# Rotary embedding on one core: the last load in two halves, and GpSimd's first store held until the first half has landed

## The chip, the cores and the metric

The kernel runs on one core of a Trainium2 chip. The metric is the device time of one execution in microseconds (us), as the median of a few executions. The profile shows the core's engines: VectorE (DVE), ScalarE (ACT), GpSimd (POOL), SyncE (SP), and 16 DMA engines that copy between HBM and the on-chip memory SBUF.

## The reference

```python
def reference(x, freqs, positions):          # x: (8, 8, 1024, 64) float32
    half = x.shape[-1] // 2
    angles = np.outer(positions, freqs)
    cos, sin = np.cos(angles), np.sin(angles)
    x_first, x_second = x[..., :half], x[..., half:]
    out_first = x_first * cos - x_second * sin
    out_second = x_first * sin + x_second * cos
    return np.concatenate([out_first, out_second], axis=-1).astype(np.float32)
```

It reads 16.8 MB and writes 16.8 MB, with a handful of operations per element.

## The kernel before

The input is cut into 8 tiles of 128 partitions, each partition with C = 64 rows of 64 numbers. GpSimd loads each tile with one DMA that turns float32 into bf16 on the way. VectorE makes four operations per tile, and GpSimd stores the bf16 result with one DMA that turns it back into float32. All these DMAs go through one queue, q0. Two small pieces travel as float32 over SyncE's hardware queue: the first 16 rows of tile 0 and the last 16 rows of tile 7.

```python
    for g in range(ntiles):                                   # 8 loads, queued at once
        lo = 0 if g else head
        nc.gpsimd.dma_start(out=xts[g][:, lo:], in_=hbm(x, g, lo))
    ...                                                       # sin and cos tables
    for g in [1, 0] + list(range(2, ntiles)):
        hi = C if g < ntiles - 1 else C - tail
        ot = opool.tile([P, C, d], bf16, name="ot")[:, :hi]
        rotate(g, 0, hi, ot)                                  # four VectorE operations
        ots.append(ot)
        nc.gpsimd.dma_start(out=hbm(out, g, 0, hi), in_=ot)   # 8 stores, in the same queue
    ...
    for r in range(0, tail, piece):                           # the last 16 rows, by SyncE
        ...
            sp.dma_start(out=hbm(out, ntiles - 1, lo, lo + piece), in_=last[:, r:r + piece])
```

## Time and profile before

| | |
|---|---|
| time, median | 85.18 us (85.12 to 85.28, 3 runs) |
| span of the profiled execution | 83.4 us |
| share of the 16 DMA engines' time taken by q0 | 95.0% |
| VectorE busy | 61.9 us (74%) |
| loads, stores as seen by the engines | 218 GB/s of bf16, 430 GB/s of float32 |

How to read it: the busiest compute engine is idle for a quarter of the span, and the DMA engines are idle only at its two ends.

The trace records every packet that a DMA engine moved, with start and length. A software DMA over 128 partitions gives each of the 16 engines 8 data packets and one packet of 4 bytes that raises the semaphore. Sorted by time, the 4-byte packets of q0 fall into groups of 16, one group for each DMA. The last of a group belongs to the **slowest engine**, and the distance from group to group is what the DMA cost on it. The records carry no engine number: the slowest engine is the last of 16, and a "mean gap" is the mean start of the first 16 store packets less the mean end of the 16 semaphore packets before them.

### The profile page before, as it was taken

How to read it: one execution, taken by the hardware profiler on the slowest of the kernel's cores; microseconds unless marked ns; L12 is line 12 of the kernel's file. 1: busy time of each engine (PE TensorE's matmuls, PEld its weight loads, DVE VectorE, ACT ScalarE, POOL GpSimd, SP SyncE). 2: the span in 40 equal slices, each digit the busy share in tenths (PEclk: the TensorE clock that was granted, in tenths of full speed). 3: DMA queues.
4: the chain of work that ended last, by engine and by line, in shares of the span. 5: the costliest groups of instructions: out<-in, count | busy, mean ns of one | idle time of the engine just before them, and what ended most of it. 6: DMA issues, size and time to landing. Idle time of an engine off the chain costs nothing.

```text
span 83.4 us, 149 instructions
## 1 busy us (share of the span) xinstructions
DVE 61.9 (74%) x48; ACT 9.3 (11%) x6; POOL 8.7 (10%) x20
## 2 busy tenths in 40 slices
DVE  1023996079999999999999999999999999500000
ACT  0000049999000000000000000000000000000000
POOL 4960000000000210000200200200200202000000
DMA  0799999999999999999999999999999999999991
GB/s 0 180 205 250 237 209 220 220 193 228 208 232 208 220 220 193 228 208 232 200 385 432 393 464 401 472 409 448 432 393 464 401 479 401 448 432 417 413 384 44
DMA packets 2920, 25.44 MB, mean 305 GB/s; under 512 B 344, under 2 KB 360, under 8 KB 1000
## 3 DMA queue, kind: packets, MB, share of 16 engines
q0 software_dynamic: 2304, 24.38, 95.0%
q1 hardware_dynamic: 576, 1.05, 3.8%
q10 hardware_dynamic: 40, 0.01, 0.1%
HBM read 16.79 MB, written 16.78 MB: 403 GB/s over the span
## 4 chain that ended last, share of the span: by engine, by line
DVE 53%; issue 13%; DMA 12%; ACT 7%; SPq 1%; DVEq 1%; ACTq 0%
DVE ot L113 20%; DMA x<-in_x_dram 12%; DVE t L112 11%; DVE ot L115 11%; DVE ot L114 8%; ACT sin_h L97 2%; ACT L97 2%; ACT L102 2%; DVE last L113 1%; ACT xt L102 1%; DVE last L114 1%; SPq L56 1%; DVEq L166 1%; ACTq L102 0%
## 5 line engine op out<-in xcount | busy, mean ns | idle before, releaser
L112 DVE TENSOR_TENSOR t<-xt,sin_h 128x4096 bf16<-128x4096 bf16 (+2 forms) x9 | 18.3, 2046 | 3.4 <-ACT sin_h L97 3.4
L113 DVE TENSOR_TENSOR ot<-xt,cos_h 128x4096 bf16<-128x4096 bf16 (+1 forms) x8 | 17.6, 2214 | 0.0
L124 POOL DMA_DIRECT2D out_dram<-ot x8 | 4.2, 526 | 60.7 <-DVE ot L115 60.7
L115 DVE TENSOR_TENSOR ot<-ot,t 128x2048 bf16<-128x2048 bf16 (+1 forms) x8 | 9.5, 1182 | 0.0
L114 DVE TENSOR_TENSOR ot<-ot,t 128x2048 bf16<-128x2048 bf16 (+1 forms) x8 | 9.5, 1182 | 0.0
L75 POOL DMA_DIRECT2D xt<-in_x_dram x8 | 4.3, 579 | 0.8 <-PEq L166 0.8
L77 DVE LOAD_MASK_SELECT pos_i<-pos_i x1 | 0.0, 14 | 3.8 <-DMA pos_i<-in_positions_dram 3.8
L102 ACT ACT_TABLE_LOAD x1 | 1.3, 1283 | 11.6 <-DMA x<-in_x_dram 11.6
L88 DVE TENSOR_TENSOR turns<-pos_f,fturn 128x2048 f32<-128x2048 f32 x1 | 2.3, 2293 | 0.0
L94 DVE TENSOR_TENSOR turns<-turns,whole 128x2048 f32<-128x2048 f32 x1 | 2.3, 2293 | 0.0
L100 ACT ACTIVATE cos_h<-whole,half_pi 128x2048 bf16<-128x2048 f32 x1 | 2.0, 2002 | 0.0
L97 ACT ACTIVATE sin_h<-turns 128x2048 bf16<-128x2048 f32 x1 | 1.9, 1909 | 0.0
L99 ACT ACTIVATE whole<-turns 128x2048 f32<-128x2048 f32 x1 | 1.9, 1893 | 0.0
L78 DVE LOAD_MASK_SELECT fr<-fr x1 | 0.0, 14 | 2.0 <-DMA fr<-in_freqs_dram 2.0
L97 ACT ACT_TABLE_LOAD x1 | 1.3, 1283 | 0.0
L92 DVE TENSOR_SCALAR whole<-turns 128x2048 f32<-128x2048 f32 x1 | 1.2, 1227 | 0.0
L113 DVE TENSOR_TENSOR last<-xt,cos_h 128x1024 f32<-128x1024 bf16 x1 | 1.2, 1214 | 0.0
L102 ACT CAST xt<-x 128x1024 bf16<-128x1024 f32 x1 | 1.0, 1045 | 0.0
L63 DVE MEMSET pos_i<- 128x128 int32 x1 | 0.2, 165 | 0.8 <-PEq L155 0.8
L114 DVE TENSOR_TENSOR last<-last,t 128x512 f32<-128x512 f32 x1 | 0.7, 692 | 0.0
L115 DVE TENSOR_TENSOR last<-last,t 128x512 f32<-128x512 f32 x1 | 0.7, 684 | 0.0
L77 DVE STREAM_SHUFFLE pos_i<-pos_i 128x128 int32<-128x128 int32 x1 | 0.3, 297 | 0.0
(9 smaller groups left out, 1.2 us busy)
## 6 DMA issues: line engine op xcount, KB each, us to landing
out_dram<-ot POOLq DMA_DIRECT2D x7, 2048.0 KB, 16.3
xt<-in_x_dram POOLq DMA_DIRECT2D x7, 1024.0 KB, 25.1
out_dram<-ot POOLq DMA_DIRECT2D x1, 1536.0 KB, 11.0
xt<-in_x_dram POOLq DMA_DIRECT2D x1, 768.0 KB, 7.6
x<-in_x_dram SPq DMA_DIRECT2D x2, 256.0 KB, 6.9
out_dram<-last SPq DMA_DIRECT2D x2, 256.0 KB, 4.5
pos_i<-in_positions_dram ACTq DMA_DIRECT2D x1, 8.0 KB, 3.7
fr<-in_freqs_dram ACTq DMA_DIRECT2D x1, 0.5 KB
```

Source lines behind the costliest of these rows:

```text
L75: nc.gpsimd.dma_start(out=xts[g][:, lo:], in_=hbm(x, g, lo))
L88: nc.vector.tensor_mul(out=turns, in0=pos_f.to_broadcast([P, C, half]), in1=fturn.to_broadcast([P, C, half]))
L94: nc.vector.tensor_sub(out=turns, in0=turns, in1=whole)
L97: nc.scalar.activation(out=sin_h, in_=turns, func=Sin, scale=twopi)
L99: nc.scalar.activation(out=whole, in_=turns, func=mybir.ActivationFunctionType.Abs)
L100: nc.scalar.activation(out=cos_h, in_=whole, func=Sin, scale=-twopi, bias=half_pi)
L102: nc.scalar.copy(out=xts[0][:, :head], in_=x0)
L112: v.tensor_mul(out=t, in0=xt, in1=sin_h[:, lo:hi, None, :].to_broadcast(pair))
L113: v.tensor_mul(out=ot, in0=xt, in1=cos_h[:, lo:hi, None, :].to_broadcast(pair))
L114: v.tensor_sub(out=ot[:, :, 0], in0=ot[:, :, 0], in1=t[:, :, 1])
L115: v.tensor_add(out=ot[:, :, 1], in0=ot[:, :, 1], in1=t[:, :, 0])
L124: nc.gpsimd.dma_start(out=hbm(out, g, 0, hi), in_=ot)
```

## The change

The intent: reads and writes are kept apart. No store is to stand in the queue while loads run, and the first half of the last load serves as the signal to queue the stores in time, while the second half still keeps the engines busy.

```diff
     for g in range(ntiles):
-        lo = 0 if g else head
-        nc.gpsimd.dma_start(out=xts[g][:, lo:], in_=hbm(x, g, lo))
+        cuts = [0 if g else head, C] if g < ntiles - 1 else [0, C // 2, C]
+        for lo, hi in zip(cuts, cuts[1:]):
+            nc.gpsimd.dma_start(out=xts[g][:, lo:hi], in_=hbm(x, g, lo, hi))
...
+    nc.gpsimd.keepalive_nop(ins=[nc.gpsimd.lower_ap(xts[-1][:, :C // 2])])
...
-        nc.gpsimd.dma_start(out=hbm(out, g, 0, hi), in_=ot)
+        tc.keep_in_program_order(nc.gpsimd.dma_start(out=hbm(out, g, 0, hi), in_=ot))
```

`keepalive_nop` is an instruction that does nothing but wait until its operand is ready.

## The prediction

> **What bounds the kernel now.** I read the page first: the totals, the strip of 40 slices and the queues.
>
> ```profile
> span 83.4 us, 149 instructions
> DVE 61.9 (74%) x48; ACT 9.3 (11%) x6; POOL 8.7 (10%) x20
> DMA  0799999999999999999999999999999999999991
> GB/s 0 180 205 250 237 209 220 220 193 228 208 232 208 220 220 193 228 208 232 200 385 432 393 464 401 472 409 448 432 393 464 401 479 401 448 432 417 413 384 44
> q0 software_dynamic: 2304, 24.38, 95.0%
> ```
>
> VectorE (DVE) is the busiest compute engine with 74%, but the DMA row is at 9 from the third slice to the last but one, and the queue that GpSimd fills (q0) takes 95% of the 16 DMA engines' time. The GB/s row doubles at slice 20 because the bytes are counted on the SBUF side: loads write bf16 there, stores read bf16 but write twice that to HBM, and the loads' rate there is half. The windows view, cut at that place, says it in two lines (columns: stretch, length, DVE, ACT and POOL busy with counts, clock, DMA share, GB/s):
>
> ```profile
> 3.40:42.40 39.00, 31.99 (x24) 9.32 (x6) 3.74 (x8) 1.00 1.03 218
> 42.40:80.40 38.00, 29.69 (x22) 0.00 (x0) 2.61 (x5) 1.00 1.06 430
> ```
>
> The share is 1.03 in the load half and 1.06 in the store half: full in both (a packet's record overlaps its neighbour's a little, hence over 1). 218 GB/s of bf16 is 436 GB/s of f32 at HBM, and the stores run at 430. So there are 77 us in which 16 engines copy without a pause, some 2.9 us before the first software packet and 3 us after the last.
>
> The timeline shows who feeds this stream (start, length, engine, line, what):
>
> ```profile
> 1.27 4.28 POOL L75 DMA_DIRECT2D xt<-in_x_dram  x8 [0.83 <-PEq L166]
> ...
> 28.64 0.54 POOL L124 DMA_DIRECT2D out_dram<-ot  x1 [23.09 <-DVE ot L115]
> 30.91 0.53 POOL L124 DMA_DIRECT2D out_dram<-ot  x1 [1.73 <-DVE ot L115]
> ...
> 39.41 2.28 DVE L113 TENSOR_TENSOR ot<-xt,cos_h 128x4096 bf16<-128x4096 bf16 x1
> 39.78 0.52 POOL L124 DMA_DIRECT2D out_dram<-ot  x1 [8.34 <-DVE ot L115]
> ...
> 69.96 0.52 POOL L124 DMA_DIRECT2D out_dram<-ot  x1 [3.49 <-DVE ot L115]
> ...
> 77.39 1.23 SPq L137 DMA_DIRECT2D out_dram<-last  x2
> ```
>
> All eight loads are queued by 5.6 us. The first store is queued at 28.64, the second at 30.91, the third at 39.78, and all of them wait in the same queue behind loads. The packet records of the trace say when: the last load's packets start up to 42.20, the first store's from 42.48 to 42.82, each engine going from its last load packet to its first store packet with only a 22 ns semaphore packet between. From landing to landing (last of the 16 increments), the loads come every 4.85 to 4.90 us (33.40, 38.27), then 43.19 for the last load (4.92) and 48.08 for the first store (4.89). So **the turn from loads to stores costs at most about 0.05 us today**. Three packets just before it took 0.86 to 0.91 us instead of 0.625, but they belong to engines that were ahead, so the slowest engine hardly shows it.
>
> The chain of waits on the page names VectorE for 53% and that is misleading here: it steps back from the last instruction over engines, and queue time behind other transfers is not a step. VectorE ends at about 72 us and its last store to q0 is queued at 69.96, while q0's packets of that store start at 76.49: 6.5 us of slack.
>
> **What the Trainium skill says.** "DMA: Bandwidth & Descriptors", section "Where 436 GB/s comes from", gives 435.2 GB/s as the ceiling of the 16 engines; 436 at the HBM side of the loads and 430 for the stores agree, so the stream has no room to go faster. The same page, "Latency and other measured facts", puts the first byte of a software-issued DMA at about 1 us. This trace bounds it: the first load's issue begins at 1.27, its first packet starts at 3.35, so 2.08 us from the start of the issue; but the engines were then busy with the first 16 packets of the hardware queue, so 2.08 is an upper limit, and the page's 1 us after 0.53 us of issue, about 1.5, a lower estimate. "Why a DMA increments its semaphore by 16 and not by 1" says every engine posts one increment as the last descriptor of a DMA; the trace has 256 four-byte packets in q0 for 16 DMAs, which agrees, at 22 ns each in the load half. "SBUF — State Buffer", section "SBUF: two separate sides", warns that VectorE can lock GpSimd out while it writes descriptors; the trace shows 0.52 us for the issue at 39.78 in the middle of a 2.28 us VectorE multiply, no longer than the 0.54 to 0.64 us of the first loads beside a mostly idle VectorE, so nothing of it is seen.
>
> **The change part by part.**
>
> 1. One more load DMA. On GpSimd it is one more issue of about 0.58 us at some 5.6 us (or a few us later, if it has to wait for a semaphore that an earlier load still uses), at a time when more than 30 us of loads are queued: beside other work, worth 0. On the engines the same bytes come as 16 packets of 4 KB (SBUF side) in place of 8 of 8 KB. Packet start to packet start is 606 ns at 8192 bytes and, in the last store, 454 ns at three quarters of the size: 606 / 4 = 151.5 and 454 / 3 = 151.3, so a packet's time is proportional to its bytes and has no visible fixed part. Half-size packets cost 303 each, nothing extra. One more semaphore packet: **+0.02 us**, on the path.
>
> 2. The wait. The last load's stream begins per engine from 37.30 to 37.95, where the load before it ends; that one's last increment is at 38.27. The first half needs 8 x 303 + 22 = 2.45 us, so it lands fully at 38.27 + 2.45 = **40.72**. GpSimd goes on 0.1 to 0.3 us later (the trace has 0.11 from the landing of the positions to VectorE, 0.29 from VectorE's end to the issue at 28.64): 40.8 to 41.0. Three stores are ready by then (28.3, 30.6, 39.4), and all go out in 3 x 0.53 = 1.6 us. The first data of the first store come 1.5 to 2.1 us after its issue starts: between **42.3 and 43.1**.
>
> 3. What covers it. The second half keeps the engines busy until 42.48 to 42.82, plus 0.02. So the bubble on the slowest engine, the one that sets the end, is between 0 and 0.25 us; on the fastest, which waits longest, it is up to 0.6, but that only takes its lead away. I take **+0.1 us**.
>
> 4. What it can win. If stores queued early do disturb the loads (the three long packets), holding them back gives back at most the 0.05 us above: **-0.03 us**.
>
> 5. Downstream. All stores after the first two have slack: the third is ready at 39.4 and due at about 52, and the last 6.5 us before it is due. The tail (the last two hardware stores, which start when q0 runs empty) moves along unchanged. The program-order pins name the order that the stores have already.
>
> Sum: 85.18 + 0.02 + 0.1 - 0.03 = **85.3 us**.
>
> **The rivals.**
>
> A. The wait opens a real bubble. For it: descriptors must now be made with 1.7 us to spare, not 14. If an idle software queue needs more than the 2.08 us that I call the limit, or the multiply that runs until 41.7 does hold the descriptors back, all 16 engines stand still up to 1 to 2 us: 86.2 to 87. Or the wait turns out to cover the whole tile: then GpSimd wakes at 43.3, the first store moves at 44.9 to 45.4, the bubble is 2.4 us and the time 87.5. Against: the 0.52 us issue under the multiply, and the change's own range of 32 rows.
>
> B. Keeping stores out of the queue speeds the loads up, which must be the intent. For it: the 0.9 us packets at 41 us. Against: the rate is the same before and after 28.64, when the first store enters the queue (landings every 4.85 to 4.90 us), and is at the ceiling; a gain of 2% would need 1.7 us and nothing in the load half is that slow. It makes 85.1.
>
> C. VectorE becomes the bound, since the schedule is made anew and its order may change. Against: 6.5 us of slack at the end and 12 us at the third store. It leaves 85.2 to 85.3.
>
> **Range and chances.** Most of the weight lies at a bubble between 0 and 0.4 us, so 85.1 to 85.6; runs of the same kernel spread by 0.16, and A has a tail upward. I take 85.0 to 85.9 as the range. Slower by over 2% needs a bubble of 1.7 us, which only A's worse forms give: 5%. Faster by over 2% has no place to come from: 1%.
>
> **What would show it.** Right: the DMA row stays at 9 through slices 18 to 21; q0 has 2448 packets (144 more); the first store is issued at 40.8 to 41.0 with three issues back to back; in windows of half a microsecond from 42 to 43.5 the share dips by less than half a slice; landings of stores stay 4.87 us apart. Wrong: a store issue after 41.5, an issue longer than 0.6 us, no packet of q0 for over half a microsecond on all engines, loads landing less than 4.8 us apart, or a VectorE that ends after 76 us.

## The result, and the profile after

The changed kernel takes **85.35 us** (85.31 to 85.44, 4 runs) beside 85.17 us (85.12 to 85.28, 4 runs) of the kernel before. The ratio is 1.0021 with a 95% interval of 1.0004 to 1.0038.

The page of the changed kernel, the same lines as were shown of before:

```profile
span 83.5 us, 151 instructions
...
DVE 61.8 (74%) x48; ACT 9.3 (11%) x6; POOL 9.2 (11%) x21
...
DMA  0999999999999999999999999999999999999991
...
q0 software_dynamic: 2448, 24.38, 95.3%
```

The packets rose from 2304 to 2448, the 144 of one more DMA, and the bytes stayed. At this grain the DMA row shows no gap. The windows of the changed kernel (stretch, length, busy time of three engines, clock, DMA share, GB/s) hardly move either:

```profile
3.40:42.40 39.00, 32.50 (x24) 9.32 (x6) 3.65 (x8) 1.00 1.03 217
42.40:80.40 38.00, 29.10 (x22) 0.00 (x0) 3.21 (x7) 1.00 1.06 428
```

The store stretch carries 428 GB/s in place of 430. The timeline of the changed kernel shows what became of the issues:

```profile
9.12 0.52 POOL L76 DMA_DIRECT2D xt<-in_x_dram  x1 [3.57 <-DMA xt<-in_x_dram]
...
38.81 2.28 DVE L114 TENSOR_TENSOR ot<-xt,cos_h 128x4096 bf16<-128x4096 bf16 x1
41.02 2.28 DVE L113 TENSOR_TENSOR t<-xt,sin_h 128x4096 bf16<-128x4096 bf16 x1
41.41 1.58 POOL L128 DMA_DIRECT2D out_dram<-ot  x3 [31.78 <-DVE ot L114]
...
69.36 0.52 POOL L128 DMA_DIRECT2D out_dram<-ot  x1 [3.49 <-DVE ot L116]
...
77.60 1.23 SPq L141 DMA_DIRECT2D out_dram<-last  x2
```

The ninth load goes out at 9.12, since it waits for the first load's landing, and that is early enough. Three stores go out together from 41.41 on. The profile puts GpSimd's wait down to VectorE's line 114, which ended at 41.10. A view names the semaphore that came last before the instruction, and here that misleads: the wait that was added is at line 119, and the view of that line has it (kind, count, length in ns, time of the first and last):

```profile
L119 POOLq EVENT_SEMAPHORE  x1: 17/17/17, 40.8 to 40.8; - x1
```

So GpSimd had its signal at 40.8 (the last of the 16 increments of the first half is at 40.74 in the trace), and its store started 0.67 us after the landing. Around the turn, in windows of half a microsecond, the kernel before has

```profile
42.00:42.50 0.50, 0.50 (x1) 0.00 (x0) 0.00 (x0) 1.00 0.56 147
42.50:43.00 0.50, 0.50 (x1) 0.00 (x0) 0.00 (x0) 1.00 1.13 459
```

and the changed kernel

```profile
42.00:42.50 0.50, 0.50 (x1) 0.00 (x0) 0.50 (x2) 1.00 0.48 90
42.50:43.00 0.50, 0.50 (x1) 0.00 (x0) 0.49 (x1) 1.00 1.25 500
```

Both dip, because a packet is counted where it starts and the two rows straddle the turn, so this view alone proves little. It has 90 GB/s in place of 147 in the first window: in the kernel before, fast engines are already storing there. The packet records say it without that doubt. Before, the engines' first store packets start on average 0.00 us after the end of their last load packet. In the changed kernel the average gap is 0.25 us: the first engine was done with its loads at 42.05, and no store packet starts before 42.53.

### The profile page after: what moved, and what is told of

It is laid out like the page before. It is cut to its first block, busy times and chain, and to the rows that moved or that the text cites. A ratio compares the mean times of both kernels' runs of the same rounds, so it can differ in the third digit from the quotient of the medians.

```text
span 83.5 us, 151 instructions
## 1 busy us (share of the span) xinstructions
DVE 61.8 (74%) x48; ACT 9.3 (11%) x6; POOL 9.2 (11%) x21
## 3 DMA queue, kind: packets, MB, share of 16 engines
q0 software_dynamic: 2448, 24.38, 95.3%
## 4 chain that ended last, share of the span: by engine, by line
DVE 53%; issue 12%; DMA 11%; ACT 7%; SPq 1%; DVEq 1%; ACTq 0%
DVE ot L114 20%; DMA x<-in_x_dram 11%; DVE t L113 11%; DVE ot L116 11%; DVE ot L115 8%; ACT sin_h L98 2%; ACT L98 2%; ACT L103 2%; DVE last L114 1%; ACT xt L103 1%; DVE last L115 1%; SPq L56 1%; DVEq L170 1%; ACTq L103 0%
## 5 line engine op out<-in xcount | busy, mean ns | idle before, releaser
L76 POOL DMA_DIRECT2D xt<-in_x_dram x9 | 4.8, 573 | 4.4 <-DMA xt<-in_x_dram 3.6
```

Source lines behind the costliest of these rows:

```text
L76: nc.gpsimd.dma_start(out=xts[g][:, lo:hi], in_=hbm(x, g, lo, hi))
```

## The experiments

Ten runs were made, two of them repeats. The first four share a chip and the runs of the kernel before, the next three another set, the last three a third. Expected texts that speak of "late by 0.6 us on one engine" go back to one engine of the changed kernel's trace whose first store packet started some 0.6 us after most others'.

| run | median us | before, us | ratio (95%) |
|---|---|---|---|
| changed kernel again | 85.34 | 85.14 | 1.0023 (1.0008 to 1.0038) |
| split only | 85.18 | 85.14 | 1.0002 (0.9989 to 1.0015) |
| hold only | 85.04 | 85.14 | 0.9985 (0.9974 to 0.9997) |
| cut at 16 rows | 85.21 | 85.14 | 1.0010 (0.9996 to 1.0024) |
| wait for the whole load | 87.77 | 85.24 | 1.0305 (1.0282 to 1.0329) |
| cut at 48 rows | 86.79 | 85.24 | 1.0196 (1.0167 to 1.0225) |
| busier VectorE | 85.15 | 85.24 | 0.9999 (0.9976 to 1.0022) |
| hold only, again | 85.12 | 85.23 | 0.9988 (0.9976 to 0.9999) |
| pins only | 85.19 | 85.23 | 1.0000 (0.9988 to 1.0012) |
| hold earlier | 85.21 | 85.23 | 0.9993 (0.9980 to 1.0006) |

My theory was that the small loss is **late descriptors**: the stores' descriptors come when some engines have run dry. The rivals were noise, the split as such, and the hold as such.

### The changed kernel again

No edit.

> The changed kernel once more, as the yardstick for the three that share this chip. Theory T (late descriptors): 85.35 us, ratio to before about 1.002, the first store issued 0.65 to 0.7 us after the first half has landed, and in the packet records the slowest engine takes about 5.1 us from its last load to the end of its first store in place of 4.84. Rival N (noise: the 0.18 us was the chip of the day): the interval holds 1.000.

It came out at 1.0023, and the interval excludes 1. The loss of 0.2 us is real. The store was issued 0.67 us after the landing again (40.56, 41.23), and the slowest engine needed 5.19 us for the first store in place of 4.84. The profiled execution was the fastest of the six, 85.12 us, and so no slower than the kernel before: what became of the 0.35 us in it is told under "Downstream" below.

### Split only

```diff
-    nc.gpsimd.keepalive_nop(ins=[nc.gpsimd.lower_ap(xts[-1][:, :C // 2])])
```

> The load in two halves, without GpSimd's wait. Theory T: the halves cost one more semaphore packet and a trace of packet time, 0.05 us in the records (2 x 2.458 against 4.867), and the turn costs nothing, since stores are queued long before: 85.2 us, ratio 1.000 to 1.001. Rival S (the split is what costs: 17 DMAs, more packets): 85.35, the same as the full change.

85.18 us, ratio 1.0002. In the records the two halves take 2 x 2.458 us against 4.867, so 0.05 us more, and the stores start without a gap (mean 0.00). The rival that blames the split falls: its 1.002 lies outside the interval. The split's own 0.05 us is below what these rounds resolve.

### Hold only

The load stays whole, and GpSimd waits for the load before it.

```diff
-        cuts = [0 if g else head, C] if g < ntiles - 1 else [0, C // 2, C]
+        cuts = [0 if g else head, C]
-    nc.gpsimd.keepalive_nop(ins=[nc.gpsimd.lower_ap(xts[-1][:, :C // 2])])
+    nc.gpsimd.keepalive_nop(ins=[nc.gpsimd.lower_ap(xts[-2])])
```

> The last load whole, and GpSimd waits for the load before it (landed at 38.2 us) ahead of its first store, so the hold is there and the store descriptors still come 3 us before they are needed. Theory T: issue at 38.9, no idle engine at the turn, 85.17 us, ratio 1.000. Rival H (holding stores back costs or wins by itself, by the order of descriptors in the queue or by undisturbed loads): loses the 0.18 us too, or comes in under 85.1.

The timeline of this kernel names the releaser rightly, and the stores go out more than 3 us before any engine is dry:

```profile
38.87 1.58 POOL L128 DMA_DIRECT2D out_dram<-ot  x3 [33.32 <-DMA xt<-in_x_dram]
```

The time is 85.04 us, ratio 0.9985. That the hold loses by itself is refuted. That it wins a little was not my expectation, so it was run again below.

### Cut at 16 rows

```diff
-        cuts = [0 if g else head, C] if g < ntiles - 1 else [0, C // 2, C]
+        cuts = [0 if g else head, C] if g < ntiles - 1 else [0, C // 4, C]
-    nc.gpsimd.keepalive_nop(ins=[nc.gpsimd.lower_ap(xts[-1][:, :C // 2])])
+    nc.gpsimd.keepalive_nop(ins=[nc.gpsimd.lower_ap(xts[-1][:, :C // 4])])
```

> The change with the cut at 16 rows in place of 32: the first part lands about 1.2 us sooner (39.5), the first store is issued at about 40.2 and its packets are ready at 41.3 to 42.0, before any engine is dry. Theory T: turn without a pause, 85.2 us, ratio 1.000 to 1.001. Rival S or H: 85.35 as with the cut at 32.

The first part landed at 39.98, later than expected, because its packets were slow on some engines (1.71 us on the slowest in place of an estimated 1.23, a quarter of 4.867 and a semaphore packet). Still the stores were in time:

```profile
40.66 1.58 POOL L128 DMA_DIRECT2D out_dram<-ot  x3 [31.05 <-DMA xt<-in_x_dram]
```

The mean gap at the turn is zero, and the first store took 4.839 us on the slowest engine, as before. The time is 85.21 us, ratio 1.0010. It points the way that late descriptors say (more than half of the loss is gone), but the interval holds both 1.000 and 1.0023, so alone this run decides nothing.

### Wait for the whole load

The load whole, and the wait moved to it: `xts[-1]` in place of `xts[-1][:, :C // 2]`, with the cuts as in "hold only".

> No split, and GpSimd's first store waits for the whole last load (landed at 43.2). Theory T: issue at 43.2 + 0.67 = 43.9, first packets 1.1 us later at 45.0 on most engines, and if one engine again gets its descriptors 0.6 us after the others, at 45.6 there: the slowest engine stands 2.2 to 2.8 us, so 87.3 to 87.9 us. If an idle software queue starts faster than that (no cost from lateness), it stays under 86.5.

87.77 us. The last increment of the load is at 43.20, and the store's issue starts at 43.88:

```profile
43.88 1.58 POOL L128 DMA_DIRECT2D out_dram<-ot  x3 [38.34 <-DMA xt<-in_x_dram]
```

Here the gap is plain in the windows too; share and GB/s in the last two columns fall to zero:

```profile
42.00:42.50 0.50, 0.50 (x1) 0.00 (x0) 0.00 (x0) 1.00 0.34 66
...
43.00:43.50 0.50, 0.50 (x2) 0.00 (x0) 0.00 (x0) 1.00 0.00 0
...
44.00:44.50 0.50, 0.50 (x2) 0.00 (x0) 0.50 (x2) 1.00 0.00 0
44.50:45.00 0.50, 0.50 (x2) 0.00 (x0) 0.50 (x2) 1.00 0.32 131
```

The first store packet starts at 44.99, which is 1.11 us after the issue began. All 16 engines start within 0.28 us, so no engine was late by 0.6 us: that part of the expectation fell, and the engine that was late by 0.6 us stands in one trace alone. The mean gap is 2.61 us, and the slowest engine lost 2.68 us in the first store (7.521 against 4.839).

### Cut at 48 rows

The change with `3 * C // 4` in place of `C // 2`, in the cuts and in the wait.

> The change with the cut at 48 rows: the first part lands about 1.2 us later (41.95), the first store is issued at 42.6, first packets at 43.7, while the engines run dry between 42.0 and 42.85. Theory T: a pause of 0.9 us on the slowest engine, 1.4 if one engine is again late: 86.1 to 86.6 us. A theory that puts the cost on the split or on the hold as such: 85.35.

86.79 us, a little over the expected range. Signal and issue are as expected (landed at 41.84, issued at 42.51):

```profile
42.51 1.58 POOL L128 DMA_DIRECT2D out_dram<-ot  x3 [33.00 <-DMA xt<-in_x_dram]
```

```profile
42.50:43.00 0.50, 0.50 (x1) 0.00 (x0) 0.49 (x1) 1.00 0.04 4
43.00:43.50 0.50, 0.50 (x2) 0.00 (x0) 0.50 (x2) 1.00 0.00 0
43.50:44.00 0.50, 0.50 (x2) 0.00 (x0) 0.50 (x2) 1.00 1.27 524
```

The first store packet starts at 43.61, once more 1.10 us after the issue began. The mean gap is 1.30 us. The slowest engine lost 1.50 us in the first store (6.341 against 4.839). What exceeds the gap is put down to slow packets of that store, which is not shown engine by engine: those that start between 45.1 and 46.0 took 0.74 to 0.92 us in place of 0.64.

### Busier VectorE

The kernel before, with two more multiplies whose results are thrown away.

```diff
         rotate(g, 0, hi, ot)
+        if g in (3, 4):
+            v.tensor_mul(out=spare, in0=xts[g], in1=cos_h ...)     # 2.28 us each
         ots.append(ot)
```

> The kernel before with two more VectorE multiplies of 2.28 us (their results are thrown away), put after the fourth and fifth tile of the loop. If the DMA stream bounds the kernel: VectorE ends at about 76.5 in place of 72.1, the last software store is issued at about 74.4, still ahead of its turn at 76.5, and the time stays at 85.2. If VectorE bounds it, as the page's chain of waits would have it (53% on VectorE): about 89.6.

The page of this kernel, with the totals and the chain of waits:

```profile
DVE 66.2 (80%) x50; ACT 9.3 (11%) x6; POOL 8.7 (10%) x20
...
DVE 63%; DMA 11%; issue 8%; ACT 7%; SPq 1%; DVEq 1%; ACTq 0%
```

VectorE does 4.3 us more, the chain of waits puts 63% on it in place of 53%, and the time is 85.15 us, as before (0.9999). The timeline shows where the 4.3 us went:

```profile
73.78 0.52 POOL L130 DMA_DIRECT2D out_dram<-ot  x1 [3.49 <-DVE ot L115]
...
77.40 1.23 SPq L143 DMA_DIRECT2D out_dram<-last  x2
```

The last software store is issued 3.8 us later than at 69.96, and SyncE's stores go out at 77.40 where they went at 77.39. The slack of VectorE took it all. The chain of waits does not show what bounds this kernel.

### Hold only, again; pins only; hold earlier

The second is the kernel before with the stores pinned in program order and nothing else. The third is the hold with `xts[-3]`, the load two before the last.

> The same program as the hold without a split, once more: there it came out at 0.9985 of the kernel before, with an interval that just misses 1. Rival H (the hold by itself wins some 0.1 us): 0.998 to 0.999 again. Rival N (noise, and no gain in the hold): the interval holds 1.000. The packet records showed no shorter stage anywhere (last load 5.107 us on the slowest engine against 4.867), so I expect N: 85.15 us.

> The kernel before with nothing of the change but the stores pinned in program order. Their order is the same already, so each theory expects 85.15 us, ratio 1.000; if the gain of the hold is real but comes from the pins, 0.9985 here too.

> The hold on the load two before the last (landed at 33.4 us), so the first two stores go out at 34.1 in place of 28.6 and 30.9. Rival H: some of the 0.1 us, between 0.9985 and 1. Rival N: 85.15 us, ratio 1.000.

The hold gives 0.9988, and again the interval just misses 1: I had expected noise, and two sets of runs speak against that. The pins give 1.0000, so they are not the source. The earlier hold gives 0.9993, whose interval holds 1 and also 0.9985. So a hold that ends in time seems to win about 0.1 us. Where it wins it, the traces do not settle. In the first hold's trace the slowest engine took longer for the last load (5.107 us against 4.867; the tail gave 0.22 us back, see "Downstream" below), in the second's it took the same 4.867; the only hint is that the second's trace is nearly free of the slow packets that the others have before the turn.

The kernel with the hold only is thus the quickest of all, by 0.1%. That is far under the 2% at which a difference is called one.

## Why the prediction was right, point by point

The prediction said 85.3 us with 85.0 to 85.9, and "the same" with 94%. Measured were 85.35 us and the same.

**The bound** was read rightly: the stream of copies, not VectorE. The busier VectorE shows by experiment that it is not VectorE; that it is the stream shows in the two slow runs, where 2.68 and 1.50 us lost in the first store became 2.5 and 1.6 us of time (87.77 and 86.79 against 85.24). One reading on the way was off. The records don't count bytes on the SBUF side but where they are written: 8192 for a load's packet and 16384 for a store's, for the same 64 rows. So the loads are beside the ceiling that the prediction cites only with what they read (2 x 218 = 436 GB/s); they write 218.

**The split** was worth 0.02 us in the prediction, 0.05 us in the records, and 0.02 us in time with an uncertainty of 0.11. The term was small and is small. The packet of half the size costs 304.5 ns, not exactly half of 606.

**The wait** has three terms, and two of them were mis-sized in opposite directions. The landing was worked out as 40.72 and was 40.74. "GpSimd goes on 0.1 to 0.3 us later" failed: in all eight traces with such a wait it is 0.67 to 0.68 us, whatever VectorE was doing; the lock that the prediction considered does not show in it. In the prediction that range came from an instruction that carries its wait itself; the ninth load is another such case, landed at 8.83 and issued at 9.12. Here the wait sits in an instruction of its own ahead of the store. The trace has that instruction at 40.77, a semaphore check of the store's line at 40.86, a second one at 41.40 and the store at 41.41, so most of the time (0.54 us) lies between the two checks. Their semaphores are those of loads that had landed by 13.9 and 18.8 us, so what fills it is not shown. "1.5 to 2.1 us after its issue starts" failed too: it is 1.10 to 1.11 us in the four traces in which an idle queue was started this way. Together they make 1.78 us from landing to first packet, where the prediction had 1.6 to 2.4, and so its 42.3 to 43.1 for the first data holds the measured 42.53. That is luck: two misses cancelled.

**The gap** was put at 0.1 us on the slowest engine, out of 0 to 0.25. The records show 0.28 us in the first trace (5.123 against 4.839) and 0.35 us in the second. The mean gap over the engines is 0.25 and 0.10 us there; the rest lies in slow packets of the first store and in the difference between the slowest engine and the mean. The mechanism was right and the size too low. The ladder of cuts shows the mechanism best: a signal at 39.98 leaves a gap of zero, at 40.74 one of 0.25, at 41.84 one of 1.30, at 43.20 one of 2.61, and the times follow: 85.21, 85.35, 86.79 and 87.77 us (ratios 1.0010, 1.0021, 1.0196 and 1.0305). The two large gaps show it beyond the noise. At the size of the change itself the ladder only agrees: the intervals of the first two overlap, so a small cost of split and hold together is not excluded.

**The gain of the hold** was put at 0.03 us from the long packets. Where nothing starves, it is 0.10 to 0.11 us (85.04 against 85.14 and 85.12 against 85.23). This term was too small. Added in the prediction's way, the measured terms give 0.05 + 0.28 - 0.10 = 0.23 us, where the time rose by 0.18 to 0.20. They come from different runs and views, so that agreement proves nothing, and the traces put another term there, the next one.

**Downstream** failed in one point: SyncE's two stores at the end do not move "along unchanged". Against the kernel before, the slowest engine of the changed kernel is 0.03 us later after the last load, 0.32 after the first store and 0.31 after q0's last packet (80.81 against 80.50), but the last packet of SyncE's stores is only 0.12 later (82.13 against 82.01), like the span (83.51 against 83.39). From q0's end on the slowest engine to the end of that tail it is 1.32 us in place of 1.51. In the repeat the tail is 1.29 us: of 0.35 us lost, 0.22 came back, and a last load that ended 0.19 earlier hid the rest. Over the twelve traces the tail is longest (1.51 us) where the engines finish q0 closest together (within 0.35 us), and shortest (1.29 us) in the three where they lie furthest apart (0.65 to 1.16 us). Why is not shown. So what the slowest engine loses alone comes back in part at the end; that the sum came to 85.3 is partly luck.

**Rival A** in its worst form was run on purpose: 87.5 us was predicted for a wait that covers the whole tile, and 87.77 was measured. **Rival B** named 85.1 us for a stream freed of stores, and the hold alone is there, but not by faster loads: the third to the seventh load together take 24.34 us on the slowest engine in all twelve traces, with stores in the queue or without. **Rival C** has no case: VectorE has its 4.3 us to spare.

**The signs.** The count of 2448 packets, the three issues in a row and the issue length of 0.53 us came as said. The issue time of 40.8 to 41.0 did not (41.41), and that named the wrong term. The share in the window from 42.0 fell to 0.48, a dip of just over half a window, where less was said; the kernel before has 0.56 there, so that was a poor sign.

Open are the source of the hold's 0.1 us and the slow packets. Every trace but that of the second hold has a stretch of about 1 us in which packets take 0.1 to 0.37 us longer. Where the stores are queued in time, it lies before the turn. In the four traces with a gap, the first store has it, 1.1 to 2.3 us after its first packet. No run takes them away, so their cause is not known.

## What to carry to other kernels

In this kernel, whose DMA engines are idle only at the two ends, holding back transfers cost up to 2.6 us and won about 0.1. So find the moment at which the queue would run dry, and have the next descriptors asked for well ahead of it: here 1.8 us passed from the signal's landing to the first packet. Choose as signal a transfer that exists already (the load before the last) rather than cut one in two for it. And before a busy engine is called the bound, give it more work and see whether the time moves.

## What the Trainium skill lacked or had wrong

- "DMA: Bandwidth & Descriptors", section "Latency and other measured facts": the first byte of a software DMA at about 1 us agrees with 1.10 to 1.11 us from the start of the issue to the first packet, in four traces. The prediction added the issue's 0.53 us to it; the page does not say from where the time counts.
- The pages that I read have no figure for GpSimd's reaction to a landing. It is 0.29 us where the DMA instruction carries the wait (landed at 8.83, issued at 9.12), and 0.67 us where a separate instruction waits ahead of it and two semaphore checks lie between.
- "DMA: Bandwidth & Descriptors", section "Queues, rings and completion order": it says that each engine goes round the queues by packets. At the start of the kernel before this agrees: from 6 to 9 us 95 packets of q0 and 95 of SyncE's queue start. At the end it does not show: SyncE's last stores were issued at 77.39, but their first packet starts at 80.10, right behind q0's first semaphore packet of the last store, and none went in between before that. At the start (issued at 0.74, first packet at 2.20) the way took 1.46 us, so the stores would have been ready by about 78.9 (an estimate). The page's packet is a run of descriptors, typically 9 to 17, and the last store has nine on each engine, so this need not contradict it; the runs don't tell.
- No page has the stretch of slow packets near the turn from loads to stores, up to 0.37 us longer each.
